# MLP scale from row tiles by ScalarE, the last slab of the down projection ordered by weights, transposes issued at half the rate

## Chip, cores, metric

One Trainium2 chip, one core. The metric is device time of one execution in microseconds (us): the median of three runs of the kernel. A change of less than about 0.2% is not told apart from none.

## What is computed

One layer of a residual block on x of 2048 tokens by 1024 channels, all in float32:

```
h = rmsnorm(x, norm_mix_pre);  proj = h @ w_in            # pool 512 | GLU 1024 | gate a 1024 | gate b 1024
merged = sigmoid(g_a) * pool_branch + sigmoid(g_b) * conv_branch
x1 = x + rmsnorm(merged @ w_o, norm_mix_post)             # "x1" in the kernel
h = rmsnorm(x1, norm_mlp_pre)
f = square(relu(h @ w_up)) @ w_down                       # w_up 1024 x 4096, w_down 4096 x 1024
out = x1 + rmsnorm(f, norm_mlp_post)
rmsnorm(x, g) = x * rsqrt(mean(x*x over channels) + 1e-6) * g
```

The change lies in the last three lines. The kernel doesn't normalise h before the up projection: it multiplies x1 itself. Since relu and square are homogeneous, the missing factor r (one number per token) appears in f as r squared, and in the last rmsnorm it only changes what stands in for the small constant: mean(f*f) + eps becomes mean(f0*f0) + e with e = eps * (mean(x1*x1) + eps)^2, up to powers of two. So the "MLP scale" e, one number per token made from the sum of x1's squares, is needed only at the very end, for the last reciprocal root.

## The kernel before

**Arithmetic.** A float32 matmul is made of three passes: each operand is split into a rounded high part (ScalarE's cast) and a low part (VectorE's subtraction), and hi x hi, hi x lo, lo x hi are summed in PSUM. Products of two-by-two blocks go by a seven-product scheme, numbered 1 to 7 in the order of the code's tables. Tokens are in two blocks, b = 0 and 1, of 1024; each has two halves t = 0, 1 of 512.

**Down projection.** The 4096 inner channels are four slabs, s = 0 to 3 (LAST = 3). A *job* is one product i of one slab for one block: 2 halves (h = 0, 1 of 24 matmuls each), 128x128 weights against 128x512 columns. `jobs` is the list in the order of execution. Each job needs the weights `w`: two sets (o = 0, 1) of a high part `wh` and a low part `wl`, in pools of three buffers each; and token cells (`tr`, `fo`, `big`). In slabs 0 to 2 the two blocks of a product stand side by side and share the weights. In the last slab all jobs of block 0 come first and then all of block 1, and each loads its weights: raw `wr` (a ScalarE cast makes `wh`) and the ready low part from DRAM, `lows`. In slabs 0 to 2 the PSUM of a half is added to an accumulator `acc` by VectorE (L120); in the last slab products that belong to the same output quarter stay in PSUM (`chains`) and are added once at their end. `ready[m, h]` tells that a quarter's accumulator is complete.

**Queues and order.** SyncE's queue (`load`, L129) issues nearly all loads, GpSimd's queue (`aside`, L133) the transposing copies and block 0's results. Each queue and each engine works in program order. Work beside the matmuls comes from generators, "lanes": `bg()` is called after each half job, and a `Lane(rate, ...)` then takes `rate` steps; a step that yields n ends its turn, and the next n - 1 calls are skipped. After `yield 2` a lane goes on two halves, one job, later. `behind()` ties the order of these steps to the matmul that was reached; high-priority blocks are scheduled earlier.

**x1 as row tiles.** x1 lies in DRAM by channels (`x1d`); the output needs tokens in rows. `turned()` (a lane of the down projection, begun with the second job) does 16 units: two loads of x1d on GpSimd's queue, one VectorE transpose (L1784), four stores to `x1t` on GpSimd's queue.

**MLP scale.** `mlp_scale` is a lane in the up projection of block 1. It loads x1d again (16 loads of 512 KB on SyncE's queue), squares on ScalarE (L579), adds on VectorE (L120), sums over partitions by 32 narrow matmuls against `inv_d` (L458) and leaves e in `floor`.

**The end.** For each block and half, a `Finish` takes the squares of each finished quarter (`squares`, ScalarE, L1811), multiplies it by the gain (`gain`, a 128x1024 VectorE multiplication at L126), makes the reciprocal root (`root`: some ten small VectorE operations) and then, for each of four row tiles, x1 + r * f in two halves (`cell`, VectorE, L1831) and stores the result (`put`). The last of the four ends, that of block 1 and t = 1, is partly done in `at_end`: at the last product its sums go half by half from PSUM (`arrive`, L120 on `rb`) and out (`leave`, L1881).

## Time and profile before

| | us |
|---|---|
| three runs | 2176.47, 2177.3, 2173.34 (median 2176.47) |
| profiled execution: time | 2174.86 |
| its span, first to last instruction | 2173.1 |
| mean granted TensorE clock | 0.995 |

The stages on that execution's time axis: mixer up to some 1236, the up projection's second block (with the MLP scale at 1307 to 1443) from 1236 to 1540, slabs 0 to 2 of the down projection from 1540 to some 2000, the last slab from there to TensorE's last matmul at 2160.2, then the end on VectorE and the last stores.

How the rows are read. A row of a stage has: from:to, length, then busy us and the number of instructions of PE (TensorE's matmuls), PEld (its weight loads, which overlap the matmuls), DVE (VectorE), ACT (ScalarE) and POOL (GpSimd), the granted clock as a share of full speed, the busy share of the DMA engines, GB/s. A row of waits has: engine, line, "<-" what it waited for, us in all, times, the longest. A row of the timeline has start, length, engine, line, operation, output<-inputs, and in brackets the idle time before it with what ended it. A row of one group has mean or min/median/max ns and shapes (partitions x elements). SPq is SyncE's queue.

### The profile page before, as it was taken

What the parts mean: (1) busy time and instruction counts of PE and PEld (TensorE: products, weight loads), DVE (VectorE), ACT (ScalarE), POOL (GpSimd) and SP (SyncE); (2) the same over time, 40 slices, a digit from 0 to 9 for tenths busy, and PEclk for the clock granted to TensorE, in tenths of its full rate; (3) what the DMA queues carried; (4) which work ended last, traced back from release to release, by engine and by line L of the source; (5) the groups of instructions that cost most, each with busy time, mean ns of one, the idle gap of its engine ahead of it and who ended that gap; (6) DMA issues with size and microseconds to landing.
All of it is one profiled execution on the core that took longest, in us unless ns stands there. A gap on an engine that the chain in (4) does not pass through costs nothing.

```text
span 2173.1 us, 25018 instructions
## 1 busy us (share of the span) xinstructions
PE 2135.3 (98%) x9424; PEld 1759.1 (81%) x9424; DVE 1716.1 (79%) x1664; ACT 1034.3 (48%) x1119; POOL 74.8 (3%) x131
## 2 busy tenths in 40 slices
PE   9999999999999999999999999999999999999996
PEld 7778888888888888888888888888887788888875
DVE  8999788999789999997777857876655775687557
ACT  6444453334534655445635766665443332223442
POOL 0000000000000000000000000000122300000000
PEclk9999999999999999999999999999999999999998
DMA  4789998688897787336686768986987775445896
GB/s 177 267 301 330 342 353 311 228 286 305 320 342 271 262 303 268 136 116 233 249 335 227 267 249 307 360 284 240 345 277 280 257 257 173 163 145 187 298 365 235
DMA packets 167498, 578.54 MB, mean 266 GB/s; under 512 B 20304, under 2 KB 24528, under 8 KB 167376
## 3 DMA queue, kind: packets, MB, share of 16 engines
q1 hardware_dynamic: 145616, 501.42, 64.4%
q10 hardware_dynamic: 12672, 46.14, 5.5%
q0 software_dynamic: 9088, 29.37, 3.9%
q8 instruction: 74, 1.21, 0.2%
q14 instruction: 48, 0.39, 0.1%
HBM read 381.20 MB, written 195.65 MB: 265 GB/s over the span
## 4 chain that ended last, share of the span: by engine, by line
PE 73%; DVE 9%; DMA 9%; issue 5%; ACT 2%; POOL 1%; SPq 0%; DVEq 0%; ACTq 0%; POOLq 0%
PE up L252 28%; PE down L1708 18%; PE wo L252 7%; PE glu L252 5%; PE B L252 4%; PE ga L252 3%; PE gb L252 3%; DVE y L910 3%; PE pool L252 2%; DMA tr<-x1d 2%; PE A L252 2%; DMA wl<-lows 1%; DMA tr<-fd 1%; POOL x1t L133 1%; DVE wl L123 1%
## 5 line engine op out<-in xcount | busy, mean ns | idle before, releaser
L252 PE MATMUL up<-big,wh 128*128 128x512 f32 x1792 | 480.9, 390 | 1.2 <-DVE big L123 0.8
L252 PEld LDWEIGHTS up<-big,wh 128*128 128x128 f32 x1792 | 335.8, 188 | 71.9 <-DVE big L123 1.1
L209 ACT CAST wh<-wr 128x1024 fp32r<-128x1024 f32 x167 | 175.5, 1052 | 314.9 <-PE up L252 68.5
L1708 PE MATMUL down<-wh,tr 128*128 128x512 f32 x784 | 307.0, 392 | 3.2 <-DVE tr L123 3.2
L910 DVE SCALAR_TENSOR_TENSOR y<-v,cst,y 128x1024 f32<-128x1024 f32 x240 | 307.0, 1279 | 2.4
L1708 PE MATMUL down<-wh,fo 128*128 128x512 f32 x776 | 298.6, 390 | 0.5 <-ACT wh L209 0.5
L252 PE MATMUL up<-big,wl 128*128 128x512 f32 x896 | 275.9, 389 | 0.0
L1708 PE MATMUL down<-wl,fo 128*128 128x512 f32 x760 | 235.1, 391 | 3.0 <-DVE wl L123 3.0
L209 ACT CAST wh<-ws 128x1024 fp32r<-128x1024 f32 x124 | 130.5, 1053 | 220.1 <-PE up L252 74.7
L252 PEld LDWEIGHTS up<-big,wl 128*128 128x128 f32 x896 | 168.2, 188 | 35.1
L1688 ACT CAST fo<-tr 128x1024 fp32r<-128x1024 f32 x86 | 90.4, 1051 | 219.2 <-DMA tr<-fd 90.8
L123 DVE TENSOR_TENSOR wl<-ws,wh 128x1024 fp32r<-128x1024 f32 x116 | 141.4, 1219 | 46.8 <-ACT wh L209 46.3
L1708 PEld LDWEIGHTS down<-wh,tr 128*128 128x128 f32 x784 | 148.0, 189 | 35.2 <-DVE tr L123 4.3
L1708 PEld LDWEIGHTS down<-wh,fo 128*128 128x128 f32 x776 | 145.9, 188 | 31.4 <-ACT wh L209 0.9
L1708 PEld LDWEIGHTS down<-wl,fo 128*128 128x128 f32 x760 | 142.7, 188 | 34.6 <-DVE wl L123 5.3
L123 DVE TENSOR_TENSOR wl<-wr,wh 128x1024 fp32r<-128x1024 f32 x111 | 135.1, 1218 | 26.0 <-ACT wh L209 22.9
L120 DVE TENSOR_TENSOR big<-big,down 128x1024 f32<-128x1024 f32 (+1 forms) x84 | 99.8, 1189 | 70.4 <-PE down L1708 70.3
L123 DVE TENSOR_TENSOR tr<-tr,fo 128x1024 fp32r<-128x1024 f32 x86 | 104.7, 1219 | 46.2 <-ACT fo L1688 46.0
L252 PE MATMUL glu<-big,wh 128*128 128x512 f32 x432 | 117.5, 393 | 3.0 <-ACT tr L408 2.5
L252 PE MATMUL wo<-big,wh 128*128 128x512 f32 x448 | 120.2, 390 | 0.0
L252 PE MATMUL gb<-big,wh 128*128 128x512 f32 x448 | 120.1, 390 | 0.0
L252 PE MATMUL ga<-big,wh 128*128 128x512 f32 x448 | 119.8, 389 | 0.0
(208 smaller groups left out, 3383.0 us busy)
## 6 DMA issues: line engine op xcount, KB each, us to landing
tr<-fd SPq DMA_DIRECT2D x110, 512.0 KB, 4.5
wr<-w_down SPq DMA_DIRECT2D x68, 512.0 KB, 6.3
wl<-kept SPq DMA_DIRECT2D x67, 512.0 KB, 5.2
kept<-wl SPq DMA_DIRECT2D x66, 512.0 KB, 5.7
wr<-w_up SPq DMA_DIRECT2D x64, 512.0 KB, 4.5
wr<-w_in SPq DMA_DIRECT2D x56, 512.0 KB, 6.0
fd<-tr ACTq DMA_DIRECT2D x54, 512.0 KB, 3.5
fd<-tr SPq DMA_DIRECT2D x48, 512.0 KB, 3.3
```

Source lines behind the costliest of these rows:

```text
L120: return nc.vector.tensor_tensor(o, a, b, op=ALU.add)
L123: return nc.vector.tensor_tensor(o, a, b, op=ALU.subtract)
L133: return nc.gpsimd.dma_start(o, src)
L209: nc.scalar.copy(hi[:, :n], src[:, :n])
L252: i = nc.tensor.matmul(ps, w[wp][:, (at + k) * P : (at + k + 1) * P], rhs[k][xp], start=start and n == 0, stop=stop and n == len(order) - ...
L910: nc.vector.scalar_tensor_tensor(acc, v[:, k : k + TB], wk, acc, op0=ALU.mult, op1=ALU.add)
L1688: nc.scalar.copy(hi, t)
L1708: i = nc.tensor.matmul(ps[gg], cells[j][xp][:, c * T + at : c * T + at + P], w[j][wp][:, c * T : (c + 1) * T], start=start and first, stop ...
```

## The change

1. `mlp_scale` and its lane in the up projection are gone. `Finish.fetch`, which loads a row tile of x1, now also squares it on ScalarE with a running sum along the row (`sx`); `root` makes e from it by two more small VectorE operations.
2. The last slab's order is by weights: products 2, 1, 6, 7, 4, each for block 0 and block 1 with one set of weights, then 5 and 3 of block 0, then 5 and 3 of block 1 with sets of their own.
3. PSUM chains are kept per block; block 1's second halves lie in two `rb` banks, which are added as two 128x512 instead of one 128x1024.
4. `turned()` waits `yield 4` instead of `yield 2` per unit: a unit comes every second job.
5. Block 0's gain multiplications run on GpSimd.
6. One lane of rate 4 does three of the four ends, from the sixth job of the last slab's list on; `last_steps` loads its row tiles between the gains.

```diff
@@ mlp_scale: 28 lines and the dictionary floor removed
...
-    DOWN_LAST = (1, 6, 7, 4, 2, 5, 3)
-    ENDS = {(0, 0): 2, (1, 0): 4, (1, 1): 5, (0, 1): 3}
+    DOWN_LAST = (2, 1, 6, 7, 4, 5, 3)
+    ENDS = {(0, 0): max((1, 2), key=DOWN_LAST.index), (1, 0): 4, (0, 1): 3, (1, 1): max((5, 7), key=DOWN_LAST.index)}
...
@@ last_product
         if i in (1, 2, 5):
-            if i == 5 and b:
-                chains[i, h] = [root_psum() if h else psum("down")[:, :T] for _ in (0, 1)]
+            tiles.pop((i, h, b), None)
+            if (i == 5 and b and h == 0) or (b and h):
+                chains[i, h, b] = [root_psum() if h else psum("down")[:, :T] for _ in (0, 1)]
             else:
-                tiles[i, h] = psum("down")
-                chains[i, h] = banks(tiles[i, h])
+                tiles[i, h, b] = psum("down")
+                chains[i, h, b] = banks(tiles[i, h, b])
...
-        if i == 5 and b:
+        if whole is None:
             for q, half in zip(ps, banks(c)):
                 mark(add(half, half, q))
...
@@ turned
-                        yield 2
+                        yield 4
...
@@ class Finish
+            self.sx = mk(p_gain, f"sx{b}{t}", F32, (P, G))
         def fetch(self, g):
             self.x[g] = mk(*BIG)
             load(self.x[g], x1t[self.b, self.t][g * P : (g + 1) * P])
+            nc.scalar.activation(junk[0], self.x[g], AF.Square, accum_out=self.sx[:, g : g + 1])
@@ gain
-            mul(two(y), two(y), row)
+            e = nc.vector if self.b else nc.gpsimd
+            e.tensor_tensor(two(y), two(y), row, op=ALU.mult)
@@ root
+            m, e = small("sm", hi - lo), small("se", hi - lo)
+            k = SQ * EPS**0.5
+            nc.vector.tensor_scalar(m, self.sx[:, lo:hi], k / D, k * EPS, op0=ALU.mult, op1=ALU.add)
+            mul(e, m, m)
+            return root_dve(ss, e, 1.0 / D)
@@ put
-            (load if self.b else aside)(out[self.b, self.t, g], self.x[g])
+            (nc.gpsimd if self.b == 0 else nc.sync).dma_start(
+                out[self.b, self.t, g], self.x[g]
+            )
@@ steps
                 self.gain(*k)
+                if len(self.x) < G:
+                    self.fetch(len(self.x))
                 yield
-            for g in range(2):
-                self.fetch(g)
             r = self.root(0, G)
-            yield lag
+            if lag:
+                yield lag
             for g in range(G):
-                if g + 2 < G:
-                    self.fetch(g + 2)
@@ last_steps
-            for g in range(G):
-                self.fetch(g)
-            for k in ((1, 0), (1, 1)):
+            for n, k in enumerate(((1, 0), (1, 1))):
                 while k not in self.ready:
                     yield 1
                 self.gain(*k)
+                yield
+                self.fetch(2 * n)
+                yield
+                self.fetch(2 * n + 1)
                 yield
...
-    jobs += [(LAST, i, b) for b in range(NB) for i in DOWN_LAST]
+    jobs += [(LAST, i, b) for i in DOWN_LAST[:5] for b in range(NB)]
+    jobs += [(LAST, i, b) for b in range(NB) for i in DOWN_LAST[5:]]
...
-    then(lambda: lanes.extend([Lane(1, scales()), Lane(1, last_weights())]), octs[1])
+    then(lambda: lanes.extend([Lane(1, last_weights())]), octs[1])
...
-                lanes += [Lane(3, fin[0, 0].steps(3), fin[0, 1].steps(3))]
-            else:
-                lanes += [Lane(2, fin[1, 0].steps(1)), Lane(2, fin[1, 1].last_steps())]
-        if s == LAST or b == 0 or (s, i) in [(0, i) for i in FIRST]:
+            if (i, b) == (DOWN_LAST[2], 0):
+                lanes += [Lane(4, fin[0, 0].steps(0), fin[1, 0].steps(0), fin[0, 1].steps(0)), Lane(2, fin[1, 1].last_steps())]
+        if (s == LAST and not (b and i in DOWN_LAST[:5])) or b == 0 or (s, i) in [(0, i) for i in FIRST]:
             w = [part(i, o) for o in (0, 1)]
```

What moves on the engines is read from the order of instructions. VectorE in the early down projection, from one transpose of x1 to the next. Between them stand the subtractions that make low parts: of weights (`wl`), of cells (`tr`), and differences of raw weights (`ws`). Before:

```order
L1784 STREAM_TRANSPOSE tr_12375<-tr_12374 128x4x8x32
L123 TENSOR_TENSOR wl_12505<-ws_12113,wh_12504 128x1024
L123 TENSOR_TENSOR ws_12664<-wr_12665,wr_12667 128x1024
L123 TENSOR_TENSOR tr_12508<-tr_12508,fo_12510 128x1024
L123 TENSOR_TENSOR wl_12661<-ws_12654,wh_12660 128x1024
L123 TENSOR_TENSOR tr_12513<-tr_12513,fo_12515 128x1024
L1784 STREAM_TRANSPOSE tr_12464<-tr_12463 128x4x8x32
```

and after:

```order
L1750 STREAM_TRANSPOSE tr_12264<-tr_12263 128x4x8x32
L123 TENSOR_TENSOR tr_12315<-tr_12315,fo_12317 128x1024
L123 TENSOR_TENSOR wl_12385<-ws_12011,wh_12384 128x1024
L123 TENSOR_TENSOR tr_12388<-tr_12388,fo_12390 128x1024
L123 TENSOR_TENSOR tr_12393<-tr_12393,fo_12395 128x1024
L123 TENSOR_TENSOR ws_12535<-wr_12536,wr_12538 128x1024
L123 TENSOR_TENSOR wl_12532<-ws_12525,wh_12531 128x1024
L123 TENSOR_TENSOR tr_12461<-tr_12461,fo_12463 128x1024
L1750 STREAM_TRANSPOSE tr_12431<-tr_12430 128x4x8x32
```

The transposes lie seven subtractions apart here where it was five: a unit every second job instead of every job.

SyncE's queue in the last slab. `wr` is a raw weight, `wl` a ready low part, `tr<-fd` a token cell, `big<-x1t` a row tile. Before, two jobs' worth:

```order
L129 DMA wl_15879<-lows_10478 128x1024
L129 DMA tr_15960<-fd_11788 128x1024
L129 DMA wr_16036<-w_down 128x1024
L129 DMA wr_16042<-w_down 128x1024
L129 DMA big_15742<-x1t_185 128x1024
L129 DMA wl_15885<-lows_11135 128x1024
L129 DMA tr_15965<-fd_12097 128x1024
L129 DMA wl_15951<-lows_10760 128x1024
L129 DMA tr_16048<-fd_11751 128x1024
L129 DMA wr_16108<-w_down 128x1024
L129 DMA wr_16114<-w_down 128x1024
L129 DMA big_15747<-x1t_185 128x1024
```

and after:

```order
L129 DMA wl_15235<-lows_10552 128x1024
L129 DMA wr_15515<-wsum_10678 128x1024
L129 DMA wr_15521<-wsum_11264 128x1024
L129 DMA tr_15249<-fd_8531 128x1024
L129 DMA tr_15306<-fd_11653 128x1024
L129 DMA tr_15311<-fd_11942 128x1024
L129 DMA wl_15241<-lows_11138 128x1024
L129 DMA tr_15382<-fd_8245 128x1024
L129 DMA wl_15373<-lows_10462 128x1024
L129 DMA wr_15648<-w_down 128x1024
L129 DMA wr_15654<-w_down 128x1024
L129 DMA tr_15387<-fd_8524 128x1024
```

Before, the four `wl`, four `wr`, two cells and two row tiles of these two jobs are queued; in the new order three `wl`, four `wr` and five cells stand in a stretch that covers two jobs and the head of the next, since one pair of `wr` and one pair of `wl` serves both blocks.

VectorE at the very end, from the last addition out of PSUM (`rb`) on. `sx` and `ss` are the row sums of squares, `sm`, `se`, `st`, `sa`, `sy`, `s` the small tiles of the reciprocal root. Before:

```order
L120 TENSOR_TENSOR big_12652<-big_12652,rb_16262 128x512
L504 SCALAR_TENSOR_TENSOR sy_16357<-s_3321_16355,sy_16349 128x2
L126 TENSOR_TENSOR tr_16379<-big_12652,ws_15183 128x512
L126 TENSOR_TENSOR s_3323_16359<-sy_16357 128x2
L120 TENSOR_TENSOR st_16410<-ss_1853_8582 128x2
L504 SCALAR_TENSOR_TENSOR s_3324_16361<-s_3323_16359,sa_16347 128x2
L492 SCALAR_TENSOR_TENSOR sa_16412<-st_16410,e_11363 128x2
L504 SCALAR_TENSOR_TENSOR sy_16363<-s_3324_16361,sy_16357 128x2
L1881 SCALAR_TENSOR_TENSOR big_15812<-big_12202,sy_16363,big_15812 128x512
L1881 SCALAR_TENSOR_TENSOR big_15812<-tr_16314,sy_16363,big_15812 128x512
L1881 SCALAR_TENSOR_TENSOR big_15814<-big_12202,sy_16363,big_15814 128x512
L1881 SCALAR_TENSOR_TENSOR big_15814<-tr_16314,sy_16363,big_15814 128x512
```

and after:

```order
L120 TENSOR_TENSOR big_12523<-big_12523,rb_16142 128x512
L504 SCALAR_TENSOR_TENSOR s_3267_16232<-s_3266_16230 128x2
L1796 TENSOR_SCALAR sm_16289<-sx_1857_8586 128x2
L126 TENSOR_TENSOR tr_16256<-big_12523,ws_15081 128x512
L126 TENSOR_TENSOR se_16290<-sm_16289 128x2
L1805 SCALAR_TENSOR_TENSOR big_16056<-big_12459,sy_16081,big_16056 128x512
L120 TENSOR_TENSOR st_16287<-ss_1856_8585 128x2
L1805 SCALAR_TENSOR_TENSOR big_16056<-big_12073,sy_16081,big_16056 128x512
L492 SCALAR_TENSOR_TENSOR sa_16293<-st_16287,se_16290 128x2
L1789 TENSOR_TENSOR big_12131<-big_12131,ws_15081 128x1024
L504 SCALAR_TENSOR_TENSOR sy_16234<-s_3267_16232,sy_16226 128x2
L126 TENSOR_TENSOR s_3269_16236<-sy_16234 128x2
```

After the last addition come now two halves of a cell of block 1's first half (L1805), a gain multiplication of 128x1024 (L1789) and the small operations of the scale, ahead of the root's end and the last eight cell halves (L1881 before, L1858 after).

GpSimd's queue after the last transposing copy, all that it does then (after; before, only eight stores of results stood here):

```order
L1789 TENSOR_TENSOR big_12777<-big_12777,ws_15081 128x1024
L1812 DMA out<-big_15420 128x1024
L1812 DMA out<-big_15426 128x1024
L1812 DMA out<-big_15698 128x1024
L1812 DMA out<-big_15729 128x1024
L1789 TENSOR_TENSOR big_12046<-big_12046,ws_15081 128x1024
L1789 TENSOR_TENSOR big_12073<-big_12073,ws_15081 128x1024
L1789 TENSOR_TENSOR big_12423<-big_12423,ws_15081 128x1024
L1789 TENSOR_TENSOR big_12459<-big_12459,ws_15081 128x1024
L1812 DMA out<-big_15940 128x1024
```

Two times four gain multiplications stand ahead of the four result stores of their half of block 0.

More of the change, by code (lines that the diff above doesn't have):

```diff
@@ L1310, in out_proj @@
         return roots(1)
-    def mlp_scale(b, buf):
-        st = None
-        for t in (0, 1):
-            sq = Squares(buf)
-            for c in range(0, CPS, 2):
-                x = [mk(*buf) for _ in (0, 1)]
-                for i in (0, 1):
-                    load(x[i], x1d[b, c + i, t])
-                yield 1
-                sq.add(x[0])
-                sq.add(x[1])
-            yield 1
-            ss = sq.total()
-            yield 2
-            if st is None:
-                st = root_psum()
-            root_acc(st, ss, inv_d, t * G)
-        yield 1
-        m = small("sa", 2 * G)
-        nc.vector.tensor_scalar(
-            m, st[:, : 2 * G], EPS, SQ * EPS**0.5, op0=ALU.add, op1=ALU.mult
-        )
-        e = p_const.tile([P, 2 * G], F32, tag=f"e{b}", name=f"e{b}")
-        mul(e, m, m)
-        for t in (0, 1):
-            floor[b, t] = e[:, t * G : (t + 1) * G]
-        yield
     def mlp_up(b, parts):
@@ L1602, in last_weights @@
             load(lows[i, o], f32(lo))
-    def scales():
-        for b in range(NB):
-            yield from mlp_scale(b, (p_fo, "fo"))
     def weights_down(s):
@@ L1886, in after @@
                     arrive(gg)
-                    if gg:
-                        r = self.root(2 * h, 2 * h + 2)
+                    if h:
+                        if gg:
+                            r = self.root(2, 4)
+                            for g in (2, 3):
+                                leave(g, r[:, g - 2 : g - 1])
+                    elif gg:
+                        r = self.root(0, 2)
                         for g in (0, 1):
-                            leave(2 * h + g, r[:, g : g + 1])
+                            leave(g, r[:, g : g + 1])
             return after
@@ L1942, in block_kernel @@
             part = weights_down(s)
-        if s == LAST and i == DOWN_LAST[0]:
+        if s == LAST and i == DOWN_LAST[0] and not b:
             part = weights_down(s)
-            if b == 0:
+        if s == LAST:
+            if (i, b) == (DOWN_LAST[0], 0):
                 gains.append(mk(p_ws, "ws"))
```

4 lines of the change are left out of this document (1 added, 3 removed).

## Prediction

> **What bounds the kernel now.** I read the page's busy shares and chain first, then the engines' busy time by stage, then TensorE's waits, then the stages with a loss.
>
> ```profile
> PE 2135.3 (98%) x9424; PEld 1759.1 (81%) x9424; DVE 1716.1 (79%) x1664; ACT 1034.3 (48%) x1119; POOL 74.8 (3%) x131
> PE 73%; DVE 9%; DMA 9%; issue 5%; ACT 2%; POOL 1%; SPq 0%; DVEq 0%; ACTq 0%; POOLq 0%
> 1236.00:1540.00 304.00, 303.25 (x1351) 251.01 (x1352) 223.79 (x198) 191.83 (x196) 1.45 (x2) 1.00 0.80 292
> 1540.00:1760.00 220.00, 213.31 (x926) 173.86 (x924) 126.89 (x109) 85.85 (x87) 59.01 (x94) 0.99 0.82 284
> 1760.00:1970.00 210.00, 209.97 (x926) 173.87 (x927) 154.01 (x134) 58.89 (x58) 0.00 (x0) 1.00 0.50 171
> 2060.00:2145.00 85.00, 76.98 (x324) 62.19 (x324) 50.19 (x68) 34.03 (x53) 4.34 (x8) 0.96 0.88 331
> 2145.00:2173.00 28.00, 15.22 (x68) 12.27 (x66) 23.89 (x60) 6.20 (x16) 0.00 (x0) 0.85 0.54 207
> PE down L1708 <- DMA wl<-lows: 8.0, 3, 6.2
> PE down L1708 <- DVE tr L123: 3.2, 2, 1.8
> PE down L1708 <- DVE wl L123: 3.0, 4, 1.3
> PE down L1708 <- ACT wh L209: 0.5, 1, 0.5
> ```
>
> TensorE bounds it: 98% busy. Work of the other engines counts only where TensorE waits for it, or behind TensorE's end. The stage rows give TensorE's pace: from 1760 to 1970 it did 926 matmuls in 210.00 us with nothing idle, 0.2268 us each. From 1540 to 1760, the stage with the transposes, it did the same 926 in 220.00: 10.0 us lost. From 2060 to 2145, 324 matmuls should take 73.5 us and took 85.00: 11.5 us lost. The four wait rows are all the waits of the down projection, 14.7 us; the rest of the 21.5 is clock:
>
> ```profile
> 1689.90:1693.80 3.90, 3.90 (x11) 2.67 (x10) 3.10 (x3) 1.85 (x2) 0.85 (x3) 0.56 0.64 226
> 2128.30:2134.00 5.70, 5.70 (x14) 4.45 (x15) 1.97 (x2) 0.68 (x2) 0.53 (x1) 0.51 0.45 183
> 2121.69 0.39 PE L1708 MATMUL down<-wh,tr 128*128 128x512 f32 x1
> 2128.25 1.22 PE L1708 MATMUL down<-wl,big 128*128 128x512 f32 x2 [6.17 <-DMA wl<-lows]
> 1687.66 0.50 PE L1708 MATMUL down<-wh,fo 128*128 128x512 f32 x1 [0.48 <-ACT wh L209]
> 1689.56 0.50 PE L1708 MATMUL down<-wh,tr 128*128 128x512 f32 x1 [1.40 <-DVE tr L123]
> 2106.00:2128.00 22.00, 16.08 (x70) 12.69 (x68) 12.45 (x15) 7.07 (x7) 1.60 (x3) 0.98 1.00 393
> ```
>
> After the one long stall (6.17 us) the granted clock is 0.51 for 5.7 us, so a stall costs more than itself: 2.8 us more here. The Trainium skill ("TensorE: Matmul & The Clock Gate", Part 1) has the clock fall after an idle window of some 3.4 us; the 6.17 us stall agrees, but the short stalls at 1687 to 1690 (0.48 and 1.40) were followed by a clock of 0.56 too, so here the measurement goes further than the page.
>
> **Part 1: the scale leaves up.** What goes, all before 1450:
>
> ```profile
> L458 PE MATMUL rb<-inv_d,fo x32: 164/250/266, 1339.5 to 1443.1; 128*128 128x1 f32 x32
> 1339.46 0.95 PE L458 MATMUL rb<-inv_d,fo 128*128 128x1 f32 x8
> 1340.27 0.96 PE L252 MATMUL up<-big,wh 128*128 128x512 f32 x3
> L579 ACT ACTIVATE fo<-fo x16: 1042/1060/1065, 1322.7 to 1437.6; 128x1024 f32<-128x1024 f32 x16
> L120 DVE TENSOR_TENSOR fo<-fo,fo x14: 1212/1219/1226, 1321.5 to 1439.3; 128x1024 f32<-128x1024 f32 x14
> L129 SPq DMA_DIRECT2D fo<-x1d x16: 319/370/1197, 1306.7 to 1421.1; - x16
> ```
>
> Eight of the 32 narrow matmuls hold TensorE from 1339.46 to 1340.27, 0.81 us; four such groups are 3.2 us, on the bounding engine: -3.2. The 16 ScalarE squares (17 us), 14 wide VectorE adds (17 us) and 16 loads of 512 KB lie beside matmuls in a stage with 0.75 us of TensorE idle in 304: worth nothing.
>
> Their replacement is 16 ScalarE squares of 128x1024 in the last slab, 1.06 us each by the row above, 17 us for a ScalarE that is busy 34.03 of 85.00 there, and that also loses ten of the weight casts (part 2): nothing, as long as no square stands ahead of an urgent cast; each waits for its row-tile load, and such a wait holds ScalarE's next cast back. The four of the last group come behind the last cast of weights.
>
> **Part 2: last slab, one load of weights for both blocks.** Five of seven products now share their weights, so the sets fall from 14 to 9, the casts (two each) from 28 to 18, raw and low-part loads from 56 to 36 of 512 KB: 10 MB less. The loss of 11.5 us here came from one thing: the queue of loads between 2106 and 2128 ran at 393 GB/s with a DMA share of 1.00, and the low part due at 2122 landed at 2128. What remains for the new order: I laid its loads against the jobs of 48 x 0.2268 = 10.9 us. Jobs of the shared products ask for 5 to 6 loads; the worst is the job that precedes the unshared products (5 of block 0): seven or eight loads and four result tiles, 12 x 0.524 = 6.3 MB, where 393 GB/s moves 4.3 MB in a job. The low part of product 3 is asked for near the end of that job, and:
>
> ```profile
> DMA to landing us min/median/max: 3.4/4.6/12.4
> L1811 ACT ACTIVATE ws<-big 128x512 f32<-128x512 f32 x32 | 20.2, 632 | 28.9 <-DVE big L120 22.8 <-DVE sy L504 2.1 <-DVE sy L499 1.9
> L126 DVE TENSOR_TENSOR big<-big,ws 128x1024 f32<-128x1024 f32 x14 | 16.9, 1220 | 5.5 <-ACT ws L1811 5.5
> L1831 DVE SCALAR_TENSOR_TENSOR big<-big,sy,big 128x512 f32<-128x512 f32 x24 | 16.7, 744 | 11.7 <-DMA big<-x1t 11.7
> L1647 ACT CAST wh<-wr 128x1024 fp32r<-128x1024 f32 x17 | 17.9, 1052 | 13.8 <-PE down L1708 13.4 <-PE rb L1708 0.4
> ```
>
> The landing row is that of the low parts. A load has 6.3 us from its free buffer to its first matmul by the order of jobs; at the median 4.6 it costs nothing, at 12.4 a stall of 6.1 and 2.8 of clock. VectorE is the other risk: two blocks' ends are now finished within the last four jobs. My count by the durations above (0.74 a cell half, 1.22 a wide addition) leaves the sum of product 3's first half ready 0.3 us ahead of the matmul that needs its bank. So I take 2 us of new stall, between 0 and 9: -11.5 + 2 = -9.5.
>
> **Part 3: transposes at half the rate.**
>
> ```profile
> POOL x1t L133 <- DVE tr L1784: 71.9, 14, 13.3
> DVE tr L1784 <- DMA tr<-x1d: 29.6, 8, 6.2
> L1784 DVE STREAM_TRANSPOSE tr<-tr x16: 1233/1245/1247, 1549.2 to 1747.7; 128x1024 f32<-128x1024 f32 x16
> 1603.25 1.25 DVE L1784 STREAM_TRANSPOSE tr<-tr 128x1024 f32<-128x1024 f32 x1 [3.70 <-DMA tr<-x1d]
> 1663.62 1.25 DVE L1784 STREAM_TRANSPOSE tr<-tr 128x1024 f32<-128x1024 f32 x1 [4.74 <-DMA tr<-x1d]
> ```
>
> Sixteen transposes in 198.5 us are 13.2 us apart, while the old code asks for one per job, 10.9 us. Of each unit's two loads one or both are queued on GpSimd behind the stores of the unit before (GpSimd waits 71.9 us for the transposes), so the chain falls behind, and VectorE, which runs in order, stands at the transposes for 29.6 us with its subtractions behind them; TensorE waits for those (the waits on tr and wl). With one unit in 21.8 us each has 8 us to spare. I take -10.0 + 1, since the first waits (3.70 at 1603) cost TensorE nothing while no lag had gathered; bounds 0 (the wait moves with the unit) and -10.0. Sixteen units from about 1536 now end near 1885, and the last slab, 14 jobs of 10.9 us before 2160, begins near 2008: nobody waits for that end.
>
> **Part 4: block 0's eight gains on GpSimd.** No such operation is in the trace. Nearest rows:
>
> ```profile
> L608 POOL CAST ident<-tr 128x128 fp32r<-128x128 f32 x1 | 0.3, 291 | 0.1
> L2034 POOL MEMSET const-float32-1.0<- 128x1 f32 x1 | 0.1, 99 | 0.0
> ```
>
> 99 ns fixed and 192 ns per 128 columns make 1.6 us for 1024 columns with one input, up to twice that with two: 1.6 to 3.1 us, against 1.22 on VectorE. I take 2.3, halfway. By the jobs' times the cells that use the last four come 6 to 10 us behind them, which covers it: nothing, and VectorE is spared 8 x 1.22. The result stores of block 0 stay on this queue, behind the multiplies; nobody waits for them.
>
> **Part 5: behind the last matmul.**
>
> ```profile
> 2159.61 0.61 PE L1708 MATMUL rb<-wl,big 128*128 128x512 f32 x2
> 2160.55 0.68 DVE L120 TENSOR_TENSOR big<-big,rb 128x512 f32<-128x512 f32 x1
> 2168.75 0.75 DVE L1881 SCALAR_TENSOR_TENSOR big<-tr,sy,big 128x512 f32<-128x512 f32 x1
> ```
>
> From the last addition to VectorE's end are 8.95 us, then 3.6 to the span's end, and VectorE has no gap in it. In the new order three more wide rows stand behind that addition: two cell halves (start to start 0.66 in the trace, 1.3), one 128x1024 gain (1.13), and small operations of the new scale (0.3): +2.7. Bounds: 0, if these run in gaps, and +5, if the finishing work of block 1 is later still.
>
> **The sum.** -3.2 - 9.5 - 9.0 + 2.7 = -19.0. Against the profiled execution's 2174.86: 2155.9. That execution lies 1.6 under the median of 2176.47; carrying the saving to the median gives 2157.5. I forecast 2157.
>
> **Rivals.**
> *B: one long stall in the last four jobs,* by the 12.4 us landing: 6.1 + 2.8 = 8.9 instead of 2, so 2164. For it: 6.3 MB asked of a job that moves 4.3. Against it: 10 MB less altogether, and before it only one of 27 loads did it.
> *C: half the rate does not free VectorE.* The transpose's load may be slow by itself, since its pieces are small; then each of the 16 units still holds VectorE, and the 9.0 of part 3 is not won: 2166. Against it: at 1698.75 and later the waits end once the pile is worked off, and the first ones hurt nobody.
> *D: GpSimd's multiplies hold VectorE up.* If a VectorE operation with two inputs in the same memory can't run beside them, the four of block 0's second half fall into the stretch where VectorE has 0.3 us of slack; each then costs its length: 4 x 2.3 = 9.2, so 2166. Slower than before from about 6 us each (4 x 6 = 24 eats the 19 and 4.4 more), then 2181 and up; at 3.1, the upper bound, it is still faster. The Trainium skill ("SBUF — State Buffer") states just such an exclusive lock between a GpSimd instruction that reads and a two-input VectorE one; no row here has the two together. "GPSIMD Engine Reference" §3.1 has 4497 ns for 2048 fp32 columns, an estimate of 2.3 us for ours.
>
> **How the numbers follow.** A 0.55 (own range 2150 to 2162: below, no stall left and no longer end make -24.7, 2152, less 2 for the spread of runs; above, the end at +5 and 3 us more of stalls), B 0.12, C 0.08, D at 2 to 3 us 0.13, D past 6 us or a like hold-up 0.07, two of B, C, D together 0.05 (near 2175). The range of 2149 to 2171 leaves out the last two and the ends of A. A measurement can tell about 0.2%, 4.4 us: faster is all of A, B, C and the mild D with 0.87, same 0.05, slower 0.08.
>
> **What would show it.** TensorE idle under 2 us from 1540 to 1900 and no clock row under 0.9 there (part 3); waits on low parts under 2 us in the last slab (part 2); no narrow matmuls in up (part 1); GpSimd's multiplies of 1.6 to 3.1 us with VectorE rows beside them of unchanged 0.74 and 1.22 (part 4, D); 11.7 us from the last addition to VectorE's end (part 5). I am wrong if the last four jobs hold a stall of over 3 us, or if VectorE's cells wait for the multiplies.

## The result and the profile after

| | before | changed |
|---|---|---|
| median of the runs | 2176.76 us (2173.34 to 2177.3, 4 runs) | 2159.73 us (2158.8 to 2162.16, 4 runs) |
| ratio | | 0.9927 (95% interval 0.991 to 0.9944) |
| profiled execution, its span | 2174.86, 2173.1 | 2162.16, 2160.4 |

The change makes the kernel 17.0 us faster; 2157 was forecast, 2149 to 2171 as the range. The page's busy line and chain of the changed kernel:

```profile
PE 2128.4 (99%) x9392; PEld 1757.4 (81%) x9392; DVE 1698.2 (79%) x1651; ACT 1027.5 (48%) x1125; POOL 95.0 (4%) x139
PE 86%; DVE 7%; DMA 4%; issue 2%; ACT 1%; SPq 0%; DVEq 0%; ACTq 0%
```

its stages:

```profile
1236.00:1540.00 304.00, 302.76 (x1339) 250.01 (x1339) 211.23 (x190) 182.27 (x186) 1.45 (x2) 1.00 0.74 270
1540.00:1760.00 220.00, 220.00 (x972) 182.23 (x971) 126.96 (x110) 88.10 (x90) 33.43 (x53) 1.00 0.74 264
2060.00:2145.00 85.00, 80.25 (x353) 65.59 (x351) 58.45 (x99) 51.07 (x98) 18.81 (x13) 1.00 0.73 273
```

and all the waits of the down projection, with one of the mixer's that is needed below:

```profile
PE down L1673 <- DVE big L120: 2.9, 1, 2.9
PE down L1673 <- DMA wl<-lows: 1.9, 1, 1.9
PE rb L458 <- DVE sm L120: 1.7, 1, 1.7
```

TensorE's share of the chain of work that ended last rises from 73 to 86%: less of that chain runs over another engine. In 1540 to 1760 it now does 972 matmuls, 46 more than before in the same time, and waits for nothing. In 2060 to 2145 it does 353 instead of 324; at the 0.2268 us of an undisturbed matmul that is 80.05 of 85.00, so 4.95 us are lost where it was 11.5.

**The two executions differ ahead of the change, too.** On every engine the order of operations is the same in both kernels up to the first matmul of the down projection (some of its products run early, in the up projection). That mark and slab 0's first matmul are rows of TensorE's timeline. Before:

```profile
1215.70 1.07 PE L1708 MATMUL down<-wh,fo 128*128 128x512 f32 x4
1539.21 0.39 PE L1708 MATMUL down<-wh,fo 128*128 128x512 f32 x1
```

and after, with TensorE's last row:

```profile
1221.50 1.07 PE L1673 MATMUL down<-wh,fo 128*128 128x512 f32 x4
1541.06 0.39 PE L1673 MATMUL down<-wh,fo 128*128 128x512 f32 x1
2144.55 0.61 PE L1673 MATMUL rb<-wl,big 128*128 128x512 f32 x2
```

VectorE's last addition and last row after:

```profile
2145.20 0.69 DVE L120 TENSOR_TENSOR big<-big,rb 128x512 f32<-128x512 f32 x1
2156.21 0.74 DVE L1858 SCALAR_TENSOR_TENSOR big<-tr,sy,big 128x512 f32<-128x512 f32 x1
```

and a stretch of the mixer after:

```profile
540.00:550.00 10.00, 8.33 (x31) 7.14 (x32) 8.34 (x13) 1.67 (x2) 0.00 (x0) 0.66 0.81 295
```

The changed kernel's profiled execution came 5.8 us later to its first down matmul (1221.50 against 1215.70); most of it is one place, 540 to 550 us, where after a wait of 1.7 us the clock was 0.66. In the fourteen profiles of this case that mark lies between 1214.84 and 1222.88, with the same instructions in the same order ahead of it. So a part of the runs' spread has nothing to do with the change, and the sizes of parts below are measured from that mark, by four differences: mark to slab 0's first matmul ("up"), from there to TensorE's end ("down"), from there to the span's end ("end"), and their sum ("rest").

| us | up | down | end | rest |
|---|---|---|---|---|
| before | 323.51 | 621.01 | 12.83 | 957.36 |
| changed | 319.56 | 604.11 | 15.22 | 938.88 |
| difference | -3.95 | -16.90 | +2.39 | -18.48 |
| forecast | -3.2 | -18.5 | +2.7 | -19.0 |

### The profile page after: what moved, and what is told of

It reads as the page before. It is cut to its first block, busy times and chain, and to the rows that moved or that the text cites. A ratio compares the mean times of both kernels' runs of the same rounds, so it can differ in the third digit from the quotient of the medians.

```text
span 2160.4 us, 24921 instructions
## 1 busy us (share of the span) xinstructions
PE 2128.4 (99%) x9392; PEld 1757.4 (81%) x9392; DVE 1698.2 (79%) x1651; ACT 1027.5 (48%) x1125; POOL 95.0 (4%) x139
## 4 chain that ended last, share of the span: by engine, by line
PE 86%; DVE 7%; DMA 4%; issue 2%; ACT 1%; SPq 0%; DVEq 0%; ACTq 0%
PE up L252 28%; PE down L1673 25%; PE wo L252 7%; PE gb L252 6%; PE glu L252 5%; PE B L252 4%; PE ga L252 4%; PE A L252 3%; PE pool L252 3%; DVE y L910 2%; PE rb L1673 1%; DMA kept<-ws 1%; DMA kept<-wl 1%; DVE tr L120 1%; DMA tr<-yd 1%
## 5 line engine op out<-in xcount | busy, mean ns | idle before, releaser
L1673 PE MATMUL down<-wh,fo 128*128 128x512 f32 x756 | 290.4, 389 | 2.9 <-DVE big L120 2.9
L1673 PE MATMUL down<-wh,tr 128*128 128x512 f32 x744 | 289.4, 389 | 0.0
L1673 PE MATMUL down<-wl,fo 128*128 128x512 f32 x740 | 227.8, 389 | 0.0
L123 DVE TENSOR_TENSOR wl<-ws,wh 128x1024 fp32r<-128x1024 f32 x116 | 141.6, 1220 | 46.7 <-ACT wh L209 46.0
L1673 PEld LDWEIGHTS down<-wh,tr 128*128 128x128 f32 x744 | 139.7, 188 | 29.0
L120 DVE TENSOR_TENSOR big<-big,down 128x1024 f32<-128x1024 f32 (+1 forms) x79 | 93.9, 1190 | 67.1 <-PE down L1673 66.7
```

Of the source, the lines that this page charges most:

```text
L120: return nc.vector.tensor_tensor(o, a, b, op=ALU.add)
L123: return nc.vector.tensor_tensor(o, a, b, op=ALU.subtract)
L1673: i = nc.tensor.matmul(ps[gg], cells[j][xp][:, c * T + at : c * T + at + P], w[j][wp][:, c * T : (c + 1) * T], start=start and first, stop ...
```

## Experiments

Twelve kernels were run. The ratio is that of runs to runs of the kernel before on the same chip; the parts are from each kernel's profile, as above.

| kernel | median us | ratio (interval) | up | down | end | rest |
|---|---|---|---|---|---|---|
| before, transposes at half the rate | 2165.19 | 0.9958 (0.9942 to 0.9973) | 323.45 | 608.64 | 12.82 | 944.92 |
| changed, transposes at the full rate | 2168.05 | 0.9973 (0.9958 to 0.9988) | 319.58 | 612.88 | 15.23 | 947.69 |
| changed, scale in up | 2160.31 | 0.9939 (0.9915 to 0.9963) | 323.46 | 603.34 | 14.62 | 941.42 |
| changed, weights loaded per job | 2163.49 | 0.9947 (0.993 to 0.9965) | 319.59 | 606.75 | 17.36 | 943.70 |
| changed, all gains on VectorE | 2156.7 | 0.9921 (0.9903 to 0.9939) | 319.61 | 602.65 | 16.37 | 938.63 |
| changed, GpSimd's gains done twice | 2165.96 | 0.996 (0.995 to 0.9971) | 319.57 | 612.83 | 15.25 | 947.64 |
| early row tiles, gains on VectorE | 2154.83 | 0.9911 (0.9892 to 0.993) | 319.57 | 603.79 | 13.34 | 936.69 |
| early row tiles, two gains on VectorE | 2157.05 | 0.9922 (0.9903 to 0.9941) | 319.55 | 605.68 | 13.16 | 938.39 |
| early row tiles, stores spread | 2157.67 | 0.9915 (0.9893 to 0.9938) | 319.63 | 605.43 | 12.25 | 937.31 |
| early row tiles, four stores left out | 2155.29 (one run) | | 319.63 | 600.31 | 13.33 | 933.27 |
| early row tiles, four stores by ScalarE | 2158.97 | 0.991 (0.9894 to 0.9926) | 319.61 | 603.63 | 16.42 | 939.65 |
| changed, once more | 2159.83 | 0.9927 (0.9904 to 0.9949) | 319.57 | 605.55 | 15.23 | 940.35 |

The last row is the control:

> The changed kernel once more, unedited, as a control beside the others on one chip: by every theory 0.7% under the kernel before, and the time from the first down matmul to the end of the span within 1 us of 938.9, whatever the part ahead of it takes (1215.7 to 1222.9 us so far).

The ratio came out the same. The rest was 940.35, 1.5 us from 938.88, so a little outside what was expected:

```profile
PE down L1673 <- DVE big L120: 4.1, 1, 4.1
PE down L1673 <- DMA wl<-lows: 0.6, 1, 0.6
```

The wait for the low part was 0.6 instead of 1.9 us and that for the addition 4.1 instead of 2.9. All of the difference lies in "down", so differences of less than some 2 us in "down" and "rest" between two profiles are not told apart here. The other two parts repeat closely: "up" is 319.55 to 319.63 in the eleven profiles without the scale in it and 323.45 to 323.51 in the three with it, and the end is 15.22 to 15.25 in four profiles: the changed kernel twice, the one with the transposes at the full rate and the one with GpSimd's gains done twice.

### The transposes

```diff
-                        yield 2
+                        yield 4
                         nc.vector.transpose(
```

The kernel before with this line alone:

> The kernel before with one edit: a transposing unit every second job instead of every job. Theory (the chain of load, transpose and store of a unit lasts some 13 us, longer than the 10.9 us between units, so VectorE stands at the transposes and TensorE waits for its subtractions): the stage from 1540 to 1760 us loses 0 to 1 us instead of 10.0, VectorE waits less than 10 us in all for the transposes' loads while they no longer pile up, the time falls by 9 to 10 us to some 2167. Rival (each unit holds VectorE by its slow load, whatever the rate): the loss only moves, time within 2 us of before.

Its stages:

```profile
1540.00:1760.00 220.00, 220.00 (x972) 182.17 (x971) 128.98 (x111) 89.69 (x91) 33.38 (x53) 1.00 0.74 264
2060.00:2145.00 85.00, 77.77 (x333) 63.08 (x332) 54.42 (x74) 34.53 (x55) 4.34 (x8) 0.96 0.87 326
```

and VectorE's wait for the transposes' loads from 1540 to 1900:

```profile
DVE tr L1784 <- DMA tr<-x1d: 3.3, 1, 3.3
```

One number of the code takes the loss of that stage away whole: 972 matmuls instead of 926, and VectorE's 29.6 us of waiting in eight waits become one of 3.3. The down projection is 12.4 us shorter; 10.0 belong to this stage, the other 2.4 lie elsewhere (324 against 333 matmuls in the row of the last slab) and are near the size by which two profiles of one kernel differ. The runs give 9.5 us (2165.19 against 2174.71 on that chip). The reverse, the changed kernel with `yield 2`:

> The changed kernel with a transposing unit every job again. Theory (the pile-up of units comes from the rate alone): the stage from 1540 to 1760 loses 9 to 11 us again, the down projection takes 613 to 615 us instead of 604.1, time 9 to 11 us more than the changed kernel. Rival (in the changed kernel part of the loss is gone with the two loads that now stand together ahead of the stores): 0 to 4 us more.

Its stage row, and two of TensorE's waits:

```profile
1540.00:1760.00 220.00, 215.50 (x940) 176.85 (x939) 131.68 (x113) 85.85 (x87) 59.06 (x94) 0.99 0.83 289
```

```profile
PE down L1673 <- DVE tr L123: 3.1, 2, 2.1
PE down L1673 <- DVE wl L123: 1.4, 2, 1.2
```

The waits on `tr` and `wl` are back: 940 matmuls, 32 fewer than the changed kernel, 7.3 us; the down projection is 8.8 us longer than the changed kernel's (7.3 than its control's), and the ratio of the runs rises from 0.9927 to 0.9973, some 10 us. That is about the 9 to 11 that were expected by the runs, slightly less by the profiles, and far above the rival's 0 to 4.

### The scale

```diff
-            nc.scalar.activation(junk[0], self.x[g], AF.Square, accum_out=self.sx[:, g : g + 1])
...
-    then(lambda: lanes.extend([Lane(1, last_weights())]), octs[1])
+    then(lambda: lanes.extend([Lane(1, scales()), Lane(1, last_weights())]), octs[1])
```

(with `mlp_scale` as before, and its e in `root`)

> The changed kernel with the MLP scale made in the up projection as before, and no squares of row tiles. Theory (the scale cost TensorE its narrow matmuls and nothing else, and the squares of the row tiles are hidden): the up projection's second block is 3.9 us longer (323.5 instead of 319.6 from the first down matmul to slab 0), the down projection stays within 1 us of 604.1, time 3 to 4 us more than the changed kernel. Rival (the squares on ScalarE hold casts and roots back in the last slab): the down projection and the end get 2 us or more shorter, time within 2 us of the changed kernel.

The up part is 323.46, as before the change: without the narrow matmuls 3.9 us are won there, and that is shown. What is left of it at the end is not. The down part is 0.8 us shorter than the changed kernel's and 2.2 shorter than its control's, the end 0.6 shorter, so the rest is only 2.5 us longer than the changed kernel's and 1.1 longer than the control's. By runs it is 0.9939 against 0.9927, some 2.6 us, with intervals that overlap. So the whole of this part is worth some 1 to 3 us, rather less than the 3 to 4 expected, and the rival, that the squares of the row tiles cost something later, is not refuted: 0.6 us of it show in the end, the rest lies within the difference of two profiles.

### The last slab: shared weights

```diff
-        if (s == LAST and not (b and i in DOWN_LAST[:5])) or b == 0 or (s, i) in [(0, i) for i in FIRST]:
+        if s == LAST or b == 0 or (s, i) in [(0, i) for i in FIRST]:
             w = [part(i, o) for o in (0, 1)]
```

> The changed kernel in its new order of jobs, but with each job of the last slab loading its own weights (28 sets of loads as before, 10 MB more). Theory (the 11.5 us lost in the last slab before came from loads: 393 GB/s and a DMA share of 1.00 while a low part was late): waits for low parts come back, 5 to 9 us in all, time 5 to 9 us more than the changed kernel. Rival (what helped is that the two blocks' ends and their row tiles are spread over the slab): within 2 us of the changed kernel.

TensorE's waits in the down projection:

```profile
PE down L1673 <- DMA wl<-lows: 2.1, 1, 2.1
PE down L1673 <- DVE big L120: 1.7, 1, 1.7
PE down L1673 <- ACT wh L1612: 1.4, 1, 1.4
```

The time comes out between the two theories, but not by the way of the first. With all 28 sets of loads back, the wait for a low part is 2.1 us, where the changed kernel has 1.9 and its control 0.6; the low part that took longest in the last slab landed after 8.9 us (9.3 in the changed kernel, 12.4 before). So most of the 8.0 us of waits for low parts before went with the new order of jobs and ends, and the 10 MB less had no measurable share in it. The old order keeps its long wait when only the transposes are changed: 6.3 us in the first experiment. What sharing does save, 3.4 to 4.8 us of the rest (against the control and the changed kernel), shows elsewhere: a slower clock behind that wait (0.68 over the five us from 2110), a wait of 1.4 us for a cast of ScalarE, which has ten more of them here, and 2.1 us at the end (VectorE's last addition starts at 2147.91, 3.8 us after TensorE's end at 2144.11, where in the changed kernel it follows at once).

Why the new order shortens the waits stays open. That the row tiles' loads no longer come in one heap does not explain it: eight of them were asked for from 2097.3 to 2114.3 before, and seven from 2093.4 to 2105.9 in this run.

### GpSimd's multiplications

VectorE (first fence), GpSimd (second) and TensorE at its two waits (third) in the last four jobs of the changed kernel; the columns are start, length, engine, line, operation, and in brackets the idle time before:

```profile
2112.38 0.75 DVE L1805 SCALAR_TENSOR_TENSOR big<-big,sy,big 128x512 f32<-128x512 f32 x1
2113.44 3.03 DVE L123 TENSOR_TENSOR tr<-tr,big 128x1024 fp32r<-128x1024 f32 x1 [0.31 <-ACT big L1653]
2116.39 6.87 DVE L1805 SCALAR_TENSOR_TENSOR big<-big,sy,big 128x512 f32<-128x512 f32 x7
2123.19 2.34 DVE L120 TENSOR_TENSOR big<-big,down 128x1024 f32<-128x1024 f32 x2
2127.52 0.69 DVE L120 TENSOR_TENSOR big<-big,down 128x512 f32<-128x512 f32 x1 [2.00 <-PE down L1673]
```

```profile
2112.55 2.84 POOL L1789 TENSOR_TENSOR big<-big,ws 128x1024 f32<-128x1024 f32 x1 [9.82 <-ACT ws L1779]
2117.94 2.79 POOL L1789 TENSOR_TENSOR big<-big,ws 128x1024 f32<-128x1024 f32 x1 [2.55 <-ACT ws L1779]
2126.05 2.42 POOL L1789 TENSOR_TENSOR big<-big,ws 128x1024 f32<-128x1024 f32 x1 [5.32 <-ACT ws L1779]
```

```profile
2112.68 0.73 PE L1673 MATMUL down<-wl,big 128*128 128x512 f32 x2 [1.88 <-DMA wl<-lows]
2124.45 0.50 PE L1673 MATMUL down<-wh,fo 128*128 128x512 f32 x1 [2.87 <-DVE big L120]
```

The subtraction at 2113.44 starts while GpSimd multiplies and ends at 2116.47, 1.1 us after the multiplication's end at 2115.39: it did nearly all of its 1.22 us of work only then. Seven cell halves that take 4.7 us alone took 6.87 beside the multiplication at 2117.94. The hold is mutual: GpSimd's 2.84 and 2.79 against 2.42 undisturbed. The addition at 2127.52, one of whose inputs is PSUM, ran in its usual 0.69 in the middle of a multiplication. So VectorE lost 1.8 + 2.2 = 4.0 us in the stretch without slack, and the addition of product 3's first half, at 2123.19, came 2.9 us late for TensorE. The Trainium skill ("SBUF — State Buffer", section "Who interferes with whom") says just that: a VectorE instruction with two inputs in SBUF, the engines' common memory, and a GpSimd one that reads SBUF exclude each other, and the order of issue decides who waits, while a VectorE instruction with at most one SBUF input does not contend unless it is in a mode that uses both of VectorE's ports. These rows agree.

The gains back on VectorE:

```diff
-            e = nc.vector if self.b else nc.gpsimd
-            e.tensor_tensor(two(y), two(y), row, op=ALU.mult)
+            mul(two(y), two(y), row)
```

> The changed kernel with block 0's eight gain multiplications back on VectorE. Theory (a GpSimd multiplication holds up two-input VectorE operations; in the profile after, a subtraction took 3.03 us instead of 1.22 and seven cell halves 6.87 instead of 4.7 beside two of them): no VectorE row is stretched, the last slab's wait of TensorE for an addition falls from 2.9 to some 1.3 us (4.0 of stretching goes, 2.4 of multiplication comes), time 1 to 2 us less than the changed kernel. Rival (VectorE is the tight engine and GpSimd's help is worth its 8 x 1.2 us): the wait grows to 4 or more, time 2 to 5 us more.

No row is stretched and no wait for an addition is left, and the down projection is 1.5 us shorter (2.9 than the control's). But the end grew by 1.15; that VectorE, with block 0's multiplications, comes later to the last product is the likely reason. Rest 938.63, ratio 0.9921: nothing that can be told from the changed kernel. Half of the expectation, then: the hold-up is gone, and the time that it cost is not won.

The opposite, each multiplication done twice (block 0's result then has the gain squared):

```diff
             e.tensor_tensor(two(y), two(y), row, op=ALU.mult)
+            if not self.b:
+                e.tensor_tensor(two(y), two(y), row, op=ALU.mult)
```

> The changed kernel with each of block 0's gain multiplications done twice on GpSimd (block 0's result then has the gain squared). Theory of the hold-up: some 2.4 us more for each of the two that fall into VectorE's full stretch, TensorE's wait for the addition grows from 2.9 to 6 to 8 us, with the slower clock behind it 4 to 7 us more time. Rival (GpSimd's multiplications are covered): within 1 us of the changed kernel.

TensorE's wait, and two small operations of VectorE beside GpSimd's multiplications:

```profile
PE down L1673 <- DVE big L120: 10.7, 2, 9.1
```

```profile
2107.88 2.31 DVE L1798 TENSOR_SCALAR sm<-sx 128x4 f32<-128x4 f32 x1
2110.42 2.25 DVE L492 SCALAR_TENSOR_TENSOR sa<-st,se 128x4 f32<-128x4 f32 x1
```

The wait is 10.7 instead of 2.9 (4.1 in the control), the rest 8.8 us longer (7.3 than the control's), more than expected: the held-up instructions here are the tiny ones of the root, four of which took 2.2 to 2.3 us instead of 0.16, one beside each of four multiplications. Among them is one with a single input (`sm<-sx`). GpSimd's time is not covered.

### The end

```diff
-                if len(self.x) < G:
-                    self.fetch(len(self.x))
+                for _ in range(1 + self.t):
+                    if len(self.x) < G:
+                        self.fetch(len(self.x))
```

together with all gains on VectorE:

> The changed kernel with block 0's gains on VectorE and the row tiles of block 0's second half asked for two at a time. In its order all cells of that half and the last gain stand ahead of the last addition; behind it only the last eight cell halves and their root are left. Theory (what stands behind the last addition sets the end, and VectorE has some 3 us with nothing to do before it): the end after TensorE's last matmul falls from 15.2 to about 13 us, no wait for an addition, time 2 to 4 us less than the changed kernel. Rival (VectorE is full from the last product on, so what is moved ahead delays the last addition as much): the end stays within 0.7 us of 15.2.

VectorE from the last addition on, without the small operations:

```profile
2141.28 0.69 DVE L120 TENSOR_TENSOR big<-big,rb 128x512 f32<-128x512 f32 x1 [0.17 <-PE rb L1673]
2142.00 0.69 DVE L126 TENSOR_TENSOR tr<-big,ws 128x512 f32<-128x512 f32 x1
2143.78 0.75 DVE L1858 SCALAR_TENSOR_TENSOR big<-big,sy,big 128x512 f32<-128x512 f32 x1
...
2150.39 0.74 DVE L1858 SCALAR_TENSOR_TENSOR big<-tr,sy,big 128x512 f32<-128x512 f32 x1
```

The three wide rows are gone from behind the addition; VectorE even waits 0.17 us for it. The end is 13.34, as forecast, and the rest 936.69, 2.2 us below the changed kernel and 3.7 below its control. Against the run with all gains on VectorE, which has the same multiplications, the end is 3.0 us shorter and the rest 1.9. 2154.83 is the lowest median of all kernels here, 0.9911 of before; its interval overlaps the changed kernel's. With six of eight gains on GpSimd:

> As the run with early row tiles, but only the two gains that fall into VectorE's full stretch (the first two of block 0's second half) are on VectorE; the other six stay on GpSimd. Theory of the exclusive hold-up: outside the full stretch GpSimd's multiplications cost nothing, and VectorE is spared six times 1.2 us, so no wait for an addition as with all gains on VectorE, and the end no longer than with them: within 1.5 us of that run. Rival (the last two multiplications collide with the cells that are now earlier): 2 us or more over that run.

VectorE beside the last two of GpSimd's multiplications, which ran from 2121.77 to 2126.52:

```profile
2123.23 0.96 DVE L120 TENSOR_TENSOR st<-ss 128x4 f32<-128x4 f32 x1 [0.71 <-ACT ws L1779]
2124.22 2.32 DVE L492 SCALAR_TENSOR_TENSOR sa<-st,se 128x4 f32<-128x4 f32 x1
```

Rest 938.39, 1.7 over the run above, which two profiles do not tell apart. The hold-up itself is there: TensorE waited 2.7 us for an addition in this kernel, against 0.8 there, and what collided with the last two multiplications was not a cell, as the rival has it, but again small operations of a root.

### The last wait for a low part

In the run with early row tiles TensorE still waits 2.2 us for a low part at product 3 of block 0, with a slower clock behind it: the next matmul takes 0.63 us instead of 0.39, and the clock is 0.75 over the five us from 2110.

```profile
2109.27 1.22 PE L1673 MATMUL down<-wl,big 128*128 128x512 f32 x2 [2.18 <-DMA wl<-lows]
2110.29 0.63 PE L1673 MATMUL down<-wh,big 128*128 128x512 f32 x1
2110.00:2115.00 5.00, 5.00 (x18) 3.95 (x17) 4.54 (x9) 2.65 (x4) 0.00 (x0) 0.75 1.02 419
```

Stage rows around that wait are set beside those of a kernel in which block 0's first half isn't stored:

> The run with early row tiles and gains on VectorE, with the four result stores of block 0's first half left out. Theory (those stores make the low part of product 3 late): no wait for a low part there. Rival (loads alone fill the queues): the wait of some 2.2 us stays.

The run with early row tiles, all stores in it:

```profile
2095.00:2110.00 15.00, 12.82 (x56) 10.31 (x55) 12.76 (x22) 9.31 (x20) 1.63 (x3) 0.97 1.00 381
```

Without the four stores:

```profile
2098.00:2113.00 15.00, 15.00 (x68) 12.41 (x67) 14.65 (x28) 11.09 (x22) 0.00 (x0) 1.00 0.91 338
```

Without the four stores TensorE does 68 matmuls in these 15 us instead of 56, the wait is gone, and the rest falls by 3.4 us, in the one profile that there is. So the loads alone do not make the wait: it takes the stores beside them. Two ways to move them did not work:

> The run with early row tiles and gains on VectorE, and the end of block 0's first half in a lane of its own that does one cell and one store per half job instead of four at once. Theory (the remaining wait for a low part, 2.2 us and as much again of slower clock at product 3 of block 0, comes from these four stores beside five loads within 8 us): that wait falls under 0.7 us, the time falls by 2 to 4 us against the run with early row tiles, to some 2152. Rival (the row tiles and weights asked for there fill the queues by themselves): the wait stays at 1.5 us or more, time within 1.5 us of that run.

```diff
-                yield
+                yield (1 if (self.b, self.t) == (0, 0) else None)
```

(in a lane of its own). Its stores were issued at 2091.33, 2092.76, 2096.32 and 2101.22, the last just beside the two low parts asked for from 2099.43: the wait grew to 4.0 us, and the rest was 937.31, no less than that of the run it started from. And from ScalarE's queue:

> The run with early row tiles and gains on VectorE, and the four result stores of block 0's first half issued from ScalarE's queue, where they stand behind the cast of weights for block 0's product 3, so after that product's low parts are asked for. Theory (a low part is late because the stores are in flight ahead of it; leaving them out took the wait away and 3.4 us, spreading them over the same time did not): the wait for a low part falls under 0.7 us, the time from the first down matmul to the end from 936.7 to 933 to 935 us, no gain undone later. Rival (the queues are full for 15 us, so the stores make the next transfer late instead, a row tile or product 5's low part, and ScalarE's casts stand behind their squares): that time stays above 936.

ScalarE issued them at 2094.23, 2095.55, 2096.88 and 2102.58, where GpSimd had issued them at 2094.21, 2095.64, 2096.86 and 2098.29: three of the four are no later, and only the last one moved. The wait was 3.1 us, the rest 939.65; the 3.0 us more than in the run with early row tiles lie in the end, 16.42, and the runs' ratio of 0.991 does not show them. This edit did not do what it was made for, so it says nothing on whether later stores would help.

## Why the prediction was right, and where it was off

The parts came out with the right signs, and most with the right mechanism; the close sum owes something to luck. By parts the measured sizes are -3.95, -6.5, -10.0 and +2.39 against -3.2, -9.5, -9.0 and +2.7: one term was 3 us too large, the three others together 2.1 us too small in what they save, and that cancels.

- **Part 1, the scale:** -3.2 forecast, -3.95 measured in up, and 323.46 again with the scale put back. Right in mechanism; the term counted the 0.81 us of a group of narrow matmuls four times; of the other 0.7 us the rows explain 0.1, since the fourth group held TensorE for 0.91. That the squares which replace it cost nothing is not shown: with them gone, down and end together were 1.4 to 2.8 us shorter, of which 0.6, at the end, is clear of what two profiles differ by.
- **Part 3, transposes:** -9.0 forecast, -10.0 in the stage. Confirmed by the one line alone and by its reverse. The residue of 1 us did not exist.
- **Part 2, last slab:** -9.5 forecast; the stage lost 4.95 instead of 11.5, so -6.5. The step that was mis-sized is "So I take 2 us of new stall": it was 4.8, of which 1.9 was the low part at the place that the count of transfers named, and 2.9 the addition of product 3's first half, for which a slack of 0.3 us was counted. The step from fewer loads to no late low part did not hold either: with all loads back in the new order the wait was 2.1 us, so it was the new order of jobs and ends that took the long wait away, which the prediction did not count.
- **Part 4, GpSimd:** "nothing" was wrong as a price; that is why the slack of 0.3 did not hold. The length of 2.3 us was right (2.4 undisturbed), but the multiplications cost VectorE 4.0 us where it was full. That VectorE's rows beside them are stretched is one of the signs by which the prediction said that it would be wrong; the other, a stall of over 3 us in the last four jobs, was just missed with 2.9 and met in the control with 4.1. Rival D, at 0.13, named this mechanism and overpriced it: 9.2 us, for four multiplications in the full stretch. Only two fell into it; the last two, from 2126.05, met a VectorE that was waiting for TensorE.
- **Part 5, the end:** 11.7 us from the last addition to VectorE's end were forecast, 2145.20 to 2156.95 is 11.75; the end grew by 2.39 against +2.7.
- **Rivals B and C:** C is refuted by the one-line run. B did not happen as one long stall; a stall of 1.9 us was there.
- **Against the runs:** the parts sum to -18.48 against -19.0, and to -17.0 with the control's profile. The median fell by 17.0, and the forecast's 2157 is missed by 2.7 us, which is within what the part ahead of the down projection takes more or less by itself.
- **The clock:** "a stall costs more than itself" held after the wait of 1.7 us at 540 (clock 0.66), after the 2.2 us in the run with early row tiles (0.75 over five us) and after the 4.1 us in the control (0.77 and 0.89 over the two stretches of five us from 2115 on), not in the changed kernel's last slab: 1.00 over 2060 to 2145 with waits of 1.9 and 2.9 us in it.

## What to carry to other kernels

A background job that is issued faster than its own chain of load, work and store can run piles up. Here that cost nothing at first; then VectorE, which works in order, stood at the transposes, and TensorE waited for the subtractions behind them. The count to make is the chain's length against the interval between two issues, here 13.2 against 10.9 us. Two multiplications handed from VectorE to GpSimd were not free where VectorE was full and read both its inputs from SBUF: they cost it 1.8 and 2.2 us, where doing one itself takes 1.2. Additions with one input in PSUM were not held. Before sizing an effect of under half a per cent, find a mark ahead of the change and measure from there, and profile the same kernel twice: what two profiles of it differ by is the least that can be called an effect.

## What was not expected of the hardware

- With the same instructions in the same order, the first 1220 us took from 1214.84 to 1222.88 us in fourteen profiles.
- The clock after a short wait is not a matter of the wait's length alone: it was 0.66 over 10 us after 1.7 us, full after 2.9, and 0.75 over five us after 2.2 in the run with early row tiles. Behind the wait of 1.7 us stand 16 matmuls of a single column, which may count as little work; behind the other two stand full matmuls. The Trainium skill ("TensorE: Matmul & The Clock Gate", Part 1) has the clock fall after an idle window of some 3.4 us, and lets that window run freely, whatever the kernel does. That the same wait may or may not be followed by a slow clock would fit a window that runs freely; a drop after 2.2 us, less than the window, is not what its rule says, and the measurement decides.
- VectorE operations of 128x4 took 2.3 us instead of 0.16 beside a GpSimd multiplication, one with a single SBUF input among them. Whether that one was in a mode that uses both ports no run here shows.
